# Engines in source order, weights split two batches ahead, metered side work, and turns on GpSimd's queue

## The chip, the core and the metric

The kernel runs on one core of a Trainium2 chip. The metric is the device time of one execution in microseconds (us). The engines are PE (TensorE, matmuls and transposes), DVE (VectorE), ACT (ScalarE), POOL (GpSimd) and SP (SyncE, which here only issues DMAs). All run their own instruction streams and wait for each other at semaphores.

## The reference

One decoder layer for 256 rows of 2048 columns, in float32:

```python
x = x + 0.5 * swiglu(rms_norm(x, ffn1_norm), gate1, up1, down1)     # 2048 -> 5632 -> 2048
h = rms_norm(x, mix_norm)
fq, fk, fv, f_logit, sq, sk, sv, mq = split(h @ w_in)
out_a = forgetting_attention(norm(fq), norm(fk), fv, log_sigmoid(f_logit + bias))  # 6 heads, causal
out_b = sliding_window_sink_attention(norm(sq), norm(sk), sv, sinks, slopes)       # 6 heads, 2 kv heads
mn = rms_norm(mem, mem_norm)
out_c = memory_attention(norm(mq), norm(mn @ w_mem_k), mn @ w_mem_v)               # 4 heads
x = x + concat(out_a, out_b, out_c) @ w_out
x = x + 0.5 * swiglu(rms_norm(x, ffn2_norm), gate2, up2, down2)
```

## The kernel before

**Projections.** Every weight matrix is read once, in batches of two K tiles (`KB = 2`) by 512 or 384 columns. A batch is loaded by a DMA of SP (`raw_`, four tiles), rounded by ACT to `hi_` and subtracted by DVE to `lo_` (three tiles each, L218 to L221), and PE forms hi x hi, hi x lo and lo x hi for two row tiles and two K tiles: 12 matmuls (`mm_rows`, L315 to L317). The two accumulators in PSUM (tag `acc`) alternate between the chunks of columns. The stages are FFN1 (chunks `ag`, `au` for gate and up, `ad` for down), the mix stage, and FFN2 (`bg`, `bu`, `bd`). The mix stage projects the memory's keys and values (`mk`, `mv`), then the columns of `w_in` in the chunks mq, sqa, skv, sqb, fqa, fka, fqb, fkb, fva, fvb, then `w_out` (`wo`).

**Side work.** After each batch `lanes.tick()` advances generators one step: a `yield n` says in how many ticks the next step comes. Two lanes hold a PSUM tile each for attention pairs (fox pairs f0, f2, f4; window pairs w0, w2, w4; memory pairs m0, m2); free generators do the rest. `heads_T` normalises the heads of a chunk (ACT squares, a chain of small DVE instructions, ACT scaling into `q_...`), transposes them with PE into the chunk's own PSUM tile (L565) and copies them out by ACT (L567). The probabilities `ss_` of a pair are transposed by PE into `pt_` (L717, L783).

**Turns.** Where a larger tile is transposed without PE (the rows of x, the hidden activations of the FFNs, the memory), DVE transposes blocks of 32 x 32 within the tile (`turn_out`, L262), four DMAs write it to DRAM (`far_`, L268), and one reads it back in the order wanted (`turn_in`). SP issues these DMAs, in one queue with the weight loads.

**Order.** Only the opening is in `tc.manual_schedule()`; from the first chunk's batch at `k == 6` on, the framework's scheduler places each engine's instructions by its own estimate of when they are ready, so a step written later can stand earlier.

Of the kernel before, what the change touches and what calls it, by code (L numbers as in the profile page):

```python
# [1 line left out]

# [31 lines left out]
class Lanes:  # L34
# [12 lines left out]
    def run(self, name, gen):  # L47
        self.free.append([name, gen, 0])

    def _step(self, item):  # L50
        item[2] -= 1
        if item[2] > 0:
            return True
        try:
            item[2] = next(item[1])
            return True
        except StopIteration:
            self.done.add(item[0])
            return False

    def tick(self):
        self.free = [i for i in self.free if self._step(i)]
        started = False
        for n in range(2):
            if self.lane[n] is None and not started:
                for q in self.queue:
                    if all(d in self.done for d in q[2]):
                        self.queue.remove(q)
                        self.lane[n] = [q[0], q[1](f"l{n}"), 0]
                        started = True  # L70
                        break
            if self.lane[n] is not None and not self._step(self.lane[n]):
                self.lane[n] = None

    def finish(self, *names):
        while not all(n in self.done for n in names):
            self.tick()
# [3 lines left out]
def hybrid_layer(ctx, tc, x, mem, ffn1_norm, ffn1_gate, ffn1_up, ffn1_down, mix_norm, mem_norm,  # L81
# [27 lines left out]
    opening = ExitStack()  # L109
    opening.enter_context(tc.manual_schedule())  # L110
# [4 lines left out]
    graw1 = cpool.tile([NK, P], F32, name="graw1")  # L115
# [15 lines left out]
    ones = cpool.tile([P, P], F32, name="ones")  # L131
    nc.gpsimd.memset(ones, 1.0)
    warm = cpool.tile([P, 1], F32, name="warm")
    nc.scalar.activation(warm, ones[:, 0:1], AF.Silu)
# [18 lines left out]
    tri = tri3[:, 0:P]  # L153
# [3 lines left out]
    def constants(tag):  # L157
# [34 lines left out]
        tc.keep_in_program_order(  # L192
            nc.vector.tensor_scalar(out=nsink6, in0=sink6, scalar1=-1.0, scalar2=None, op0=ALU.mult))
# [19 lines left out]
    def load_w(w, k0, nk, c0, width, name):  # L213
        raw = wpool.tile([P, KB, 512], F32, tag="raw", bufs=4, name=f"raw_{name}")
        hi = wpool.tile([P, KB, 512], F32R, tag="hi", bufs=3, name=f"hi_{name}")
        lo = wpool.tile([P, KB, 512], F32R, tag="lo", bufs=3, name=f"lo_{name}")
        r, h, l = (t[:, :nk, :width] for t in (raw, hi, lo))
        nc.sync.dma_start(  # L218
            r, w[k0 * P:(k0 + nk) * P, c0:c0 + width].rearrange("(k p) c -> p k c", p=P))
        nc.scalar.copy(h, r)  # L220
        nc.vector.tensor_tensor(out=l, in0=r, in1=h.bitcast(F32), op=ALU.subtract)  # L221
        return h, l

# [32 lines left out]
    def turn_out(tmp, src, name):  # L256
# [3 lines left out]
        for t in range(NT):  # L260
            tc.keep_in_program_order(
                nc.vector.transpose(  # L262
                    out=tmp.rearrange("p (t b k s) -> p t k b s", b=4, t=NT, s=32)[:, t],
                    in_=src[:, t, :].rearrange("p (k b f) -> p k b f", b=4, f=32)))
        yield 2
        far = dpool.tile([NT, 4, 32, 4, P], F32, name=f"far_{name}")
# [3 lines left out]
        yield 2  # L270
# [5 lines left out]
    def turned(dst):  # L276

        return dst.rearrange("p (c k s) -> p k c s", c=4 * NT, s=32)

    def scaled(xT, raw, k0, g0):  # L280

        rv = turned(raw)
        for k in range(4):
            g = gT[:, g0 + k0 + k:g0 + k0 + k + 1]
# [4 lines left out]
            if k % 2:  # L289
                yield 1  # L290

    def turn_chunk(xT, src, tile, k0, g0, name):
        far = yield from turn_out(tile(f"out_{name}"), src, name)
        raw = tile(f"in_{name}")
        nc.sync.dma_start(*turn_in(raw, far))
        yield 3
        yield from scaled(xT, raw, k0, g0)

    def square_sums(ss, src, c):
        for t in range(NT):  # L300
            junk = small.tile([P, 512], F32, tag="junk", bufs=2, name="junk")
            tc.keep_in_program_order(
                nc.scalar.activation(junk, src[:, t, :], AF.Square, accum_out=ss[:, t, c:c + 1]))
# [15 lines left out]
    def project(acc, aT, w, c0, width, kts, nk_all, done, name, before=None):  # L319

        for k0, n in kts:
            k = k0
            while k < k0 + n:
                b = min(KB, k0 + n - k)
                if before:
                    before(k)
                wh, wl = load_w(w, k, b, c0, width, f"{name}_{k}")
                for j in range(b):
                    mm_rows(acc, aT, k + j, wh[:, j, :], wl[:, j, :], done == 0, done == nk_all - 1)
                    done += 1  # L330
                k += b
                lanes.tick()
        return done

    def project_end(acc, aT, w, c0, k0, n, name, landed):
# [3 lines left out]
        for k in range(k0, k0 + n, KB):  # L339
            wh, wl = load_w(w, k, KB, c0, 512, f"{name}_{k}")  # L340
# [9 lines left out]
        lanes.tick()  # L350

    def project_first(acc, aT, w, x_tiles, ordered, name):
# [11 lines left out]
        def batch(k):  # L364
            if k in XLOAD:
                load_x(nc.sync, *XLOAD[k])
            return load_w(w, k, KB, 0, 512, f"{name}_{k}")

# [10 lines left out]
        lanes.tick()  # L379
        two, three = split_one(2), split_one(3)  # L380
        mm_rows(acc, aT, 2, *two, False, False)
        nxt = batch(4)
        x_tiles(4)
        mm_rows(acc, aT, 3, *three, False, False)
        lanes.tick()
        for k in range(4, NK, KB):
            (wh, wl), nxt = nxt, batch(k + KB) if k + KB < NK else None
            if k == 6:
                ordered()
# [3 lines left out]
            lanes.tick()  # L393


    def ffn(xT, before, first, stats, wg, wu, wd, after, beside, last, name):


        with tc.tile_pool(name=f"h_{name}", bufs=1, reuse_waits="tile") as hpool, \
# [68 lines left out]

    ss0 = cpool.tile([P, NT, 4], F32, name="ss0")
# [6 lines left out]
    XLOAD.update({6: (6, 2), 8: (8, 4), 10: (12, 4)})  # L476
# [11 lines left out]
    def sum_stages(ss, src, c, wait=None):  # L488
        yield 2 + c if wait is None else wait
# [13 lines left out]
    def turns_a(htmp, turn_tile):  # L503
# [3 lines left out]
        for c in range(4):  # L507
# [24 lines left out]
    ffn(x0T, None, (x_tiles, opening.close), stats0, gate1, up1, down1, after1, beside_a, False, "a")  # L532
# [3 lines left out]
    with tc.tile_pool(name="mix", bufs=1, reuse_waits="tile") as mx, \  # L536
# [3 lines left out]
        def heads_T(acc, nh, r, gi, dst, name, off=0):  # L540

            q = mt.tile([P, 4 * SEQ], F32, tag="q", name=f"q_{name}").rearrange("p (t w) -> p t w", t=NT)
            s = small.tile([P, NT, 4], F32, tag="hs", name=f"hs_{name}")
            cols = lambda h: slice(off + h * HD, off + (h + 1) * HD)
            nc.vector.memset(s, 1.0)
            for t in range(NT):
                for h in range(nh):
                    junk = small.tile([P, HD], F32, tag="junkh", bufs=2, name="junkh")
                    nc.scalar.activation(junk, acc[:, t, cols(h)], AF.Square, scale=r[:, t:t + 1],
                                         accum_out=s[:, t, h:h + 1])  # L550
                yield 1
# [4 lines left out]
            yield 2  # L556
# [4 lines left out]
            yield 2  # L561
            tv = acc.rearrange("p a b -> p (a b)")[:, :nh * SEQ].rearrange("p (h s) -> p h s", h=nh)
            for h in range(nh):
                for t in range(NT):
                    nc.tensor.transpose(tv[:, h, t * P:(t + 1) * P], q[:, t, h * HD:(h + 1) * HD], ident)  # L565
# [340 lines left out]
```

## Time and profile before

| | us |
|---|---|
| median of 3 runs (range) | 1803.91 (1803.52 to 1804.58) |
| the profiled execution | 1803.99 |
| span of its trace | 1802.3 |
| PE busy | 1792.4 |
| DVE busy | 976.4 |
| ACT busy | 845.7 |
| POOL busy | 12.1 |

The span is what the trace covers, from the first to the last instruction; the 1.7 us beyond it lie around the execution. Busy time of an engine is the sum over its instructions. The granted clock of PE is full in all slices.

### The profile page before, as it was taken

What the parts mean: (1) busy time and instruction counts of PE and PEld (TensorE: products, weight loads), DVE (VectorE), ACT (ScalarE), POOL (GpSimd) and SP (SyncE); (2) the same over time, 40 slices, a digit from 0 to 9 for tenths busy, and PEclk for the clock granted to TensorE, in tenths of its full rate; (3) what the DMA queues carried; (4) which work ended last, traced back from release to release, by engine and by line L of the source; (5) the groups of instructions that cost most, each with busy time, mean ns of one, the idle gap of its engine ahead of it and who ended that gap; (6) DMA issues with size and microseconds to landing.
All of it is one profiled execution on the core that took longest, in us unless ns stands there. A gap on an engine that the chain in (4) does not pass through costs nothing.

```text
span 1802.3 us, 21677 instructions
## 1 busy us (share of the span) xinstructions
PE 1792.4 (99%) x8170; PEld 1507.2 (84%) x8170; DVE 976.4 (54%) x1197; ACT 845.7 (47%) x1149; POOL 12.1 (1%) x31
## 2 busy tenths in 40 slices
PE   9999999999999999999999999999999999999998
PEld 7888888888888888888999888888888888888887
DVE  5555555555555564645665565555555555544443
ACT  6444444444445443656666454444444444433332
POOL 2000000000000000000000000000000000000000
PEclk9999999999999999999999999999999999999999
DMA  7777777777787777765656586777777777666663
GB/s 240 217 219 214 220 214 218 217 216 218 227 252 234 231 220 239 223 176 152 183 151 185 176 257 188 217 216 222 222 225 223 217 219 214 218 200 198 206 205 128
DMA packets 228025, 379.16 MB, mean 210 GB/s; under 512 B 13834, under 2 KB 65360, under 8 KB 227792
## 3 DMA queue, kind: packets, MB, share of 16 engines
q1 hardware_dynamic: 226512, 375.36, 68.8%
q8 instruction: 64, 1.05, 0.2%
q0 software_dynamic: 528, 1.22, 0.2%
q10 hardware_dynamic: 880, 1.19, 0.2%
q14 instruction: 41, 0.34, 0.1%
HBM read 358.31 MB, written 19.41 MB: 210 GB/s over the span
## 4 chain that ended last, share of the span: by engine, by line
PE 98%; DVE 1%; ACT 1%; DMA 0%; issue 0%; POOL 0%; DVEq 0%; POOLq 0%; ACTq 0%
PE ua L316 4%; PE ua L317 4%; PE gb L317 4%; PE ub L317 4%; PE gb L315 4%; PE ub L315 4%; PE gb L316 4%; PE ub L316 4%; PE ua L315 4%; PE da L316 4%; PE db L316 4%; PE db L315 4%; PE da L317 4%; PE db L317 4%; PE da L315 4%; PE ga L316 4%
## 5 line engine op out<-in xcount | busy, mean ns | idle before, releaser
L221 DVE TENSOR_TENSOR lo_bd<-raw_bd,hi_bd 128x1024 fp32r<-128x1024 f32 x88 | 107.7, 1224 | 122.6 <-ACT hi_bd L220 122.5
L221 DVE TENSOR_TENSOR lo_bu<-raw_bu,hi_bu 128x1024 fp32r<-128x1024 f32 x88 | 107.8, 1225 | 119.5 <-ACT hi_bu L220 119.5
L221 DVE TENSOR_TENSOR lo_au<-raw_au,hi_au 128x1024 fp32r<-128x1024 f32 x88 | 107.8, 1225 | 114.2 <-ACT hi_au L220 114.2
L221 DVE TENSOR_TENSOR lo_ad<-raw_ad,hi_ad 128x1024 fp32r<-128x1024 f32 x88 | 107.5, 1223 | 104.7 <-ACT hi_ad L220 104.6
L220 ACT CAST hi_bd<-raw_bd 128x1024 fp32r<-128x1024 f32 x88 | 92.8, 1055 | 145.5 <-PE db L317 140.5
L221 DVE TENSOR_TENSOR lo_bg<-raw_bg,hi_bg 128x1024 fp32r<-128x1024 f32 x88 | 107.4, 1220 | 96.4 <-ACT hi_bg L220 95.6
L220 ACT CAST hi_bg<-raw_bg 128x1024 fp32r<-128x1024 f32 x88 | 92.8, 1055 | 142.1 <-PE gb L317 86.5
L221 DVE TENSOR_TENSOR lo_ag<-raw_ag,hi_ag 128x1024 fp32r<-128x1024 f32 x86 | 104.9, 1220 | 93.8 <-ACT hi_ag L220 92.9
L220 ACT CAST hi_ad<-raw_ad 128x1024 fp32r<-128x1024 f32 x88 | 92.8, 1054 | 131.7 <-PE da L317 121.5
L220 ACT CAST hi_ag<-raw_ag 128x1024 fp32r<-128x1024 f32 x86 | 90.7, 1055 | 135.9 <-PE ga L317 83.2
L220 ACT CAST hi_bu<-raw_bu 128x1024 fp32r<-128x1024 f32 x88 | 92.8, 1054 | 105.2 <-PE ub L317 78.9
L220 ACT CAST hi_au<-raw_au 128x1024 fp32r<-128x1024 f32 x88 | 92.5, 1054 | 102.6 <-PE ua L317 79.1
L316 PE MATMUL da<-lo_ad,hT_a 128*128 128x512 f32 x352 | 137.0, 389 | 0.8 <-DVE lo_ad L221 0.8
L316 PE MATMUL ua<-lo_au,x0T 128*128 128x512 f32 x352 | 137.0, 389 | 0.3 <-DVE lo_au L221 0.3
L316 PE MATMUL gb<-lo_bg,x2T 128*128 128x512 f32 x352 | 137.0, 389 | 0.0
L315 PE MATMUL gb<-hi_bg,x2T 128*128 128x512 f32 x352 | 136.9, 389 | 0.0
L317 PE MATMUL ua<-hi_au,x0T 128*128 128x512 f32 x352 | 136.9, 389 | 0.0
L315 PE MATMUL da<-hi_ad,hT_a 128*128 128x512 f32 x352 | 136.9, 389 | 0.0
L317 PE MATMUL da<-hi_ad,hT_a 128*128 128x512 f32 x352 | 136.9, 389 | 0.0
L317 PE MATMUL gb<-hi_bg,x2T 128*128 128x512 f32 x352 | 136.9, 389 | 0.0
L315 PE MATMUL ub<-hi_bu,x2T 128*128 128x512 f32 x352 | 136.9, 389 | 0.0
L316 PE MATMUL ub<-lo_bu,x2T 128*128 128x512 f32 x352 | 136.9, 389 | 0.0
(478 smaller groups left out, 3934.9 us busy)
## 6 DMA issues: line engine op xcount, KB each, us to landing
raw_au<-in_ffn_up_dram SPq DMA_DIRECT2D x88, 512.0 KB, 4.5
raw_ad<-in_ffn_down_dram SPq DMA_DIRECT2D x88, 512.0 KB, 5.0
raw_bg<-in_ffn_gate_dram SPq DMA_DIRECT2D x88, 512.0 KB, 4.5
raw_bu<-in_ffn_up_dram SPq DMA_DIRECT2D x88, 512.0 KB, 4.4
raw_bd<-in_ffn_down_dram SPq DMA_DIRECT2D x88, 512.0 KB, 4.6
raw_ag<-in_ffn_gate_dram SPq DMA_DIRECT2D x86, 512.0 KB, 4.5
raw_wo<-in_w_out_dram SPq DMA_DIRECT2D x16, 512.0 KB, 5.2
far_a<-turn_out_a SPq DMA_DIRECT2D x44, 128.0 KB, 2.6
```

The source lines that it names most:

```text
L220: nc.scalar.copy(h, r)
L221: nc.vector.tensor_tensor(out=l, in0=r, in1=h.bitcast(F32), op=ALU.subtract)
L315: nc.tensor.matmul(acc[:, t, :w], hi, wh, start=first, stop=False)
L316: nc.tensor.matmul(acc[:, t, :w], hi, wl, start=False, stop=False)
L317: nc.tensor.matmul(acc[:, t, :w], lo, wh, start=False, stop=last)
```

## The change

It has five parts. (1) The whole program is in `manual_schedule()`, so each engine runs in the order in which the code is written. (2) A list `plan` holds all weight batches in order, and `weights()` loads and splits them ahead of use: one batch ahead at first, two from the first chunk's `k == 8` on. (3) The steps of side work carry estimates of their DVE and ACT cost; a tick has some room for each, by the width of the batch, and a step that would overdraw it is put off. `Slots` hands out the shared tiles, and `held_by` makes a chunk's start wait until the steps that read its accumulator are written. (4) A turn's five DMAs are issued by POOL, and the reader follows six ticks after the turn. (5) The heads of all chunks but fkb, and the probabilities of m0, m2, w0 and w2, are transposed by turns instead of PE; fkb, w4 and the fox pairs stay on PE.

```diff
     def _step(self, item):
         item[2] -= 1
-        if item[2] > 0:
+        if item[2] > 0 or any(cost and room <= -0.4 for cost, room in zip(item[3], self.room)):
             return True
+        self.room = [room - cost for cost, room in zip(item[3], self.room)]
...
-    def tick(self):
-        self.free = [i for i in self.free if self._step(i)]
+    def tick(self, room=(0.0, 0.0)):
+        self.room = [min(a + b, b) for a, b in zip(self.room, room)]
...
+        self.free = [i for i in self.free if self._step(i)]
...
-    opening = ExitStack()
-    opening.enter_context(tc.manual_schedule())
+    ctx.enter_context(tc.manual_schedule())
...
+    AHEAD = [1]
+    plan, traced = [], []
...
+    def weights(name, k):
+
+        while plan and len(traced) < 1 + AHEAD[0]:
+            traced.append((plan[0][4], plan[0][1], load_w(*plan.pop(0))))
+        got = traced.pop(0)
+        assert got[:2] == (name, k), (got[:2], name, k)
+        return got[2]
+
+    def room(width):
+        t = KB * 6 * (width + 32) / 2400
+        return t - 0.17 - 1.03e-3 * KB * width, t - 0.22 - 0.81e-3 * KB * width
...
-            nc.sync.dma_start(far[:, :, :, a, :].rearrange("t b f n -> f (t b) n"),
-                              tmp[32 * a:32 * a + 32, :].rearrange("f (c n) -> f c n", n=P))
-        yield 2
+            nc.gpsimd.dma_start(far[:, :, :, a, :].rearrange("t b f n -> f (t b) n"),
+                                tmp[32 * a:32 * a + 32, :].rearrange("f (c n) -> f c n", n=n))
         return far
 
     def turn_in(dst, far):
-        return dst.rearrange("p (t n) -> p t n", t=NT), far.rearrange("t b f a n -> (b f) t (a n)")
...
+        nt, n = far.shape[0], far.shape[4]
+        nc.gpsimd.dma_start(dst[:, 0:nt * 4 * n].rearrange("p (t n) -> p t n", t=nt),
+                            far.rearrange("t b f a n -> (b f) t (a n)"))
...
-                wh, wl = load_w(w, k, b, c0, width, f"{name}_{k}")
-                for j in range(b):
+                wh, wl = weights(name, k)
+                for j in range(KB):
                     mm_rows(acc, aT, k + j, wh[:, j, :], wl[:, j, :], done == 0, done == nk_all - 1)
                     done += 1
-                k += b
-                lanes.tick()
+                k += KB
+                lanes.tick(room(width))
...
         for k in range(4, NK, KB):
-            (wh, wl), nxt = nxt, batch(k + KB) if k + KB < NK else None
-            if k == 6:
-                ordered()
+            if k == 8:
+                AHEAD[0] = 2
+            wh, wl = weights(name, k)
...
+        def turn(src, name, out, then=None):
+
+            i, tmp = yield from take("turn", f"turn_{name}")
+            yield 0, 0.17 + 1.05e-3 * src.shape[1] * src.shape[2], 0.0
+            turn_in(tmp, turn_out(tmp, src, name))
+            if then:
+                then()
+            yield 5
+            yield from out(tmp)
+            slots["turn"].give(i)
...
-            tv = acc.rearrange("p a b -> p (a b)")[:, :nh * SEQ].rearrange("p (h s) -> p h s", h=nh)
-            for h in range(nh):
-                for t in range(NT):
-                    nc.tensor.transpose(tv[:, h, t * P:(t + 1) * P], q[:, t, h * HD:(h + 1) * HD], ident)
+            if not by_pe:
+                lanes.done.add(f"{name}.acc")
             yield 1
-            nc.scalar.activation(dst, tv, AF.Copy, scale=gT[:, G_HEAD + gi:G_HEAD + gi + 1])
+            if by_pe:
+                tv = acc.rearrange("p a b -> p (a b)")[:, :nh * SEQ].rearrange("p (h s) -> p h s", h=nh)
+                for h in range(nh):
+                    for t in range(NT):
+                        nc.tensor.transpose(tv[:, h, t * P:(t + 1) * P], q[:, t, h * HD:(h + 1) * HD], ident)
+                slots["q"].give(iq)
+                yield 1, 0.0, 0.8
+                nc.scalar.activation(dst, tv, AF.Copy, scale=gain)
+                lanes.done.add(f"{name}.acc")
+                return
+
+            def out(tmp):
+                yield 0, 0.0, 0.8
+                nc.scalar.activation(dst.rearrange("p h (c s) -> p h c s", s=32), turned(tmp, NT, nh), AF.Copy,
+                                     scale=gain)
+
+            yield from turn(q, name, out, lambda: slots["q"].give(iq))
...
+        held_by = [("mk.acc",), ("mv",)]
 
         def chunk(c0, width, name):
+            lanes.finish(*held_by[-2])
             acc = psum("acc", name)
             project(acc, x1T, w_in, c0, width, [(0, NK)], NK, 0, name)
+            held_by.append(("sv", "sk.acc") if name == "skv" else (name if name[:2] == "fv" else f"{name}.acc",))
             return acc
```

The probabilities by DMA use the same `turn` (`turn_p`), followed by an ACT copy back into `ss_`.

What the change does to the order shows at three places. The first is PE in chunk fqb, between two weight batches (`hi_fqb`, `lo_fqb`; x1T are the normalised rows). Before, the six transposes of fka's heads stand there:

```order
L315 MATMUL fqb<-hi_fqb_7309,x1T 128x384
L316 MATMUL fqb<-lo_fqb_7310,x1T 128x384
L317 MATMUL fqb<-hi_fqb_7309,x1T 128x384
L565 MATMUL fka<-ident,q_fka 128x128 x6
L315 MATMUL fqb<-hi_fqb_7333,x1T 128x384
L316 MATMUL fqb<-lo_fqb_7334,x1T 128x384
L317 MATMUL fqb<-hi_fqb_7333,x1T 128x384
```

After, the batches follow each other directly:

```order
L354 MATMUL fqb<-hi_fqb_7238,x1T 128x384
L355 MATMUL fqb<-lo_fqb_7239,x1T 128x384
L356 MATMUL fqb<-hi_fqb_7238,x1T 128x384
L354 MATMUL fqb<-hi_fqb_7256,x1T 128x384
L355 MATMUL fqb<-lo_fqb_7257,x1T 128x384
L356 MATMUL fqb<-hi_fqb_7256,x1T 128x384
```

The six transposes are gone from PE, and the heads of fka go out by a turn. Over the program 78 such instructions go: eight each for mk, mq, m0 and m2, six each for sqa, sqb, fqa, fka, fqb, w0 and w2, four for sk.

The second place is PE at the heads of fkb, which stay on PE. Before, their transposes stand inside chunk fva, with 12 more matmuls of fva and 8 of a fox pair ahead of fvb:

```order
L315 MATMUL fva<-hi_fva_7743,x1T 128x384
L316 MATMUL fva<-lo_fva_7744,x1T 128x384
L317 MATMUL fva<-hi_fva_7743,x1T 128x384
L565 MATMUL fkb<-ident,q_fkb 128x128 x6
L315 MATMUL fva<-hi_fva_7767,x1T 128x384
L316 MATMUL fva<-lo_fva_7768,x1T 128x384
```

After, they stand behind the last matmul of fva, directly ahead of fvb:

```order
L354 MATMUL fva<-hi_fva_7701,x1T 128x384
L355 MATMUL fva<-lo_fva_7702,x1T 128x384
L356 MATMUL fva<-hi_fva_7701,x1T 128x384
L648 MATMUL fkb<-ident,q_fkb 128x128 x6
L354 MATMUL fvb<-hi_fvb_7744,x1T 128x384
L355 MATMUL fvb<-lo_fvb_7745,x1T 128x384
L356 MATMUL fvb<-hi_fvb_7744,x1T 128x384
```

fvb takes the accumulator that fkb held, and ACT copies fkb's transposed heads out of it (`qkv<-fkb`), so the matmuls that lay between are no longer there.

The third place is DVE at the end of FFN1's third down chunk, where it adds the chunk to x (`x_sb<-da`) and transposes x's blocks for a turn (`turn_out_x`). Before:

```order
L221 TENSOR_TENSOR lo_ad_42_4985<-raw_ad_42_4983,hi_ad_42_4984 128x1024
L221 TENSOR_TENSOR lo_ad_0_5010<-raw_ad_0_5008,hi_ad_0_5009 128x1024
L450 SCALAR_TENSOR_TENSOR x_sb<-da_4552,x_sb 128x512 x2
L262 STREAM_TRANSPOSE turn_out_x_5026<-x_sb 128x4x4x32 x2
L221 TENSOR_TENSOR lo_ad_2_5031<-raw_ad_2_5029,hi_ad_2_5030 128x1024
L221 TENSOR_TENSOR lo_ad_4_5049<-raw_ad_4_5047,hi_ad_4_5048 128x1024
```

After:

```order
L264 TENSOR_TENSOR lo_ad_0_4969<-raw_ad_0_4967,hi_ad_0_4968 128x1024
L264 TENSOR_TENSOR lo_ad_2_4987<-raw_ad_2_4985,hi_ad_2_4986 128x1024
L484 SCALAR_TENSOR_TENSOR x_sb<-da_4562,x_sb 128x512 x2
L264 TENSOR_TENSOR lo_ad_4_5012<-raw_ad_4_5010,hi_ad_4_5011 128x1024
L302 STREAM_TRANSPOSE turn_out_x_5028<-x_sb 128x4x4x32 x2
L264 TENSOR_TENSOR lo_ad_6_5038<-raw_ad_6_5036,hi_ad_6_5037 128x1024
```

The split of the next chunk's second batch (`lo_ad_2`) now stands ahead of the sum, and one more split between the sum and the block transposes.

## Rows read from the trace of the kernel before

**Rows 1.** The page: span; engines' busy us; a group: busy us, mean ns, idle.

```profile
span 1802.3 us, 21677 instructions
PE 1792.4 (99%) x8170; PEld 1507.2 (84%) x8170; DVE 976.4 (54%) x1197; ACT 845.7 (47%) x1149; POOL 12.1 (1%) x31
...
L316 PE MATMUL da<-lo_ad,hT_a 128*128 128x512 f32 x352 | 137.0, 389 | 0.8 <-DVE lo_ad L221 0.8
```

**Rows 2.** Windows: length; PE, PEld, DVE, ACT, POOL busy (count); clock; DMA share, GB/s.

```profile
200.00:400.00 200.00, 200.00 (x884) 165.62 (x883) 105.66 (x100) 88.77 (x94) 0.00 (x0) 1.00 0.72 215
...
850.00:900.00 50.00, 50.00 (x295) 48.61 (x294) 32.85 (x86) 32.61 (x84) 1.11 (x2) 1.00 0.66 184
```

**Rows 3.** The chain that ended last: start, us, what.

```profile
813.94 0.87 PE mq L565 x8
...
862.70 0.44 PE skv L565 x4
...
924.07 0.66 PE fka L565 x6
924.72 0.17 PE fqb L315
...
925.94 0.17 PE fqb L316
...
962.66 0.65 PE fkb L565 x6
```

**Rows 4.** PE's waits: line, releaser, us in total, times, longest.

```profile
PE db L345 <- DVE x_sb L450: 0.8, 1, 0.8
...
PE wo L316 <- DVE lo_wo L221: 0.6, 1, 0.6
PE sqa L316 <- DVE lo_sqa L221: 0.5, 1, 0.5
PE ua L316 <- DVE lo_au L221: 0.3, 1, 0.3
```

**Rows 5.** Timeline, 671 to 675 us: start, us, instruction, idle before it and releaser.

```profile
671.18 1.29 DVE L450 SCALAR_TENSOR_TENSOR x_sb<-da,x_sb 128x512 f32<-128x512 f32 x2 [3.01 <-PE da L317]
...
672.38 1.30 DVE L262 STREAM_TRANSPOSE turn_out_x<-x_sb 128x512 f32<-128x512 f32 x2
...
673.60 2.32 DVE L221 TENSOR_TENSOR lo_ad<-raw_ad,hi_ad 128x1024 fp32r<-128x1024 f32 x2
...
674.84 0.50 PE L316 MATMUL da<-lo_ad,hT_a 128*128 128x512 f32 x1 [0.76 <-DVE lo_ad L221]
```

**Rows 6.** Timeline, SP's DMA issues in `wo`, 1044 to 1048 us.

```profile
1044.07 0.37 SPq L295 DMA_DIRECT2D turn_in_x<-far_x  x1
...
1044.48 3.96 SPq L218 DMA_DIRECT2D raw_wo<-in_w_out_dram  x3
```

**Rows 7.** Timeline, ACT, around the transposes of fkb.

```profile
962.70 0.83 ACT L220 CAST hi_fvb<-raw_fvb 128x768 fp32r<-128x768 f32 x1 [1.25 <-PE fva L317]
...
963.44 0.90 ACT L567 ACTIVATE qkv<-fkb,gT 128x768 f32<-128x768 f32 x1
```

**Rows 8.** DMA issues: queue, count, KB each, median us to landing.

```profile
far_x<-turn_out_x SPq DMA_DIRECT2D x28, 128.0 KB, 3.1
...
turn_in_m<-far_m SPq DMA_DIRECT2D x4, 512.0 KB, 6.0
```

**Rows 9.** Groups of POOL's instructions: busy us, mean ns, idle before.

```profile
L660 POOL DMA_DIRECT2D nck_all<-nck_dram x1 | 0.6, 577 | 3.2 <-ACT junkh L549 3.2
L162 POOL DMA_DIRECT2D bias<-in_forget_bias_dram x1 | 0.6, 569 | 1.1 <-DMA graw<-in_mem_norm_dram 1.1
...
L161 POOL DMA_DIRECT2D graw<-in_fox_q_gain_dram x1 | 0.5, 487 | 0.0
```

**Rows 10.** Groups of DVE, 760 to 980 us: busy us, mean ns, idle before.

```profile
L631 DVE TENSOR_SCALAR ss_f<-ss_f,ri_f 128x256 f32<-128x256 f32 x6 | 2.1, 349 | 0.0
...
L631 DVE TENSOR_SCALAR ss_f<-ss_f,ri_f 128x128 f32<-128x128 f32 x6 | 1.7, 285 | 0.1
```

More of the change, by code (lines that the diff above doesn't have):

```diff
@@ L1 @@
-from contextlib import ExitStack
 import concourse.bass as bass
@@ L73, in tick, with __init__, take, give @@
                 self.lane[n] = None
+        self.free = [i for i in self.free if self._step(i)]
     def finish(self, *names):
         while not all(n in self.done for n in names):
-            self.tick()
+            self.tick((1.2, 1.2))
+class Slots:
+    def __init__(self, n):
+        self.n, self.asked, self.taken, self.back = n, 0, 0, set()
+    def take(self):
+        i, self.asked = self.asked, self.asked + 1
+        while self.taken < i or i >= self.n and i - self.n not in self.back:
+            yield 1
+        self.taken += 1
+        return i
+    def give(self, i):
+        self.back.add(i)
 @with_exitstack
@@ L466, in xchunk, with plan_ffn @@
         return x_sb[:, :, c * 512:(c + 1) * 512]
+    def plan_ffn(wg, wu, wd, name, first):
+        for j in range(DFF // 512):
+            for w, kind in ((wg, "g"), (wu, "u")):
+                k0 = 4 if first and j == 0 and w is wg else 0
+                plan_w(w, j * 512, 512, k0, NK - k0, f"{name}{kind}{j}")
+        for c in range(4):
+            plan_w(wd, c * 512, 512, 0, NF, f"{name}d{c}")
+    W_IN = [(MEM_Q, 512, "mq"), (FOX_F, 390, "sqa"), (SWA_K, 512, "skv"), (SWA_Q + 384, 384, "sqb")]
+    for half, a in (("a", 0), ("b", 384)):
+        W_IN += [(FOX_Q + a, 384, f"fq{half}"), (FOX_K + a, 384, f"fk{half}")]
+    W_IN += [(FOX_V, 384, "fva"), (FOX_V + 384, 384, "fvb")]
+    W_OUT = [(0, 6, 10), (1, 6, 10), (0, 0, 6), (1, 0, 6), (2, 0, 16), (3, 0, 16)]
+    plan_ffn(gate1, up1, down1, "a", True)
+    plan_w(w_mem_k, 0, 512, 0, NK, "mk")
+    plan_w(w_mem_v, 0, 512, 0, NK, "mv")
+    for c0, width, n in W_IN:
+        plan_w(w_in, c0, width, 0, NK, n)
+    for c, k0, n in W_OUT:
+        plan_w(w_out, c * 512, 512, k0, n, f"wo{c}")
+    plan_ffn(gate2, up2, down2, "b", False)
     ss0 = cpool.tile([P, NT, 4], F32, name="ss0")
@@ new lines, in by_dma, with transposes @@
+            def by_dma():
+                yield from probabilities()
+                yield 1
+                yield from turn_p(s, f"p_{name}")
+            def transposes(tag):
+                pp = psum(tag, f"pt_{name}")
+                for i in range(2):
+                    for j in range(3):
+                        nc.tensor.transpose(pp[:, i, j * P:(j + 1) * P], s[:, i, j * P:(j + 1) * P], ident)
+                yield 1, 0.0, 0.85
+                nc.scalar.copy(s, pp[:, :, 0:3 * P])
@@ L725, in values @@
+            if by_pe:
+                lanes.run(f"e_{name}", probabilities())
+                lanes.put(f"p_{name}", transposes, (f"e_{name}",))
+            else:
+                lanes.run(f"p_{name}", by_dma())
         def values(tag, h0, v, mix0, name):
@@ L790, in mem_stages @@
[L790 to L797 removed]
+                    nc.scalar.activation(part(i, t), sp[:, i, t * SEQ:(t + 1) * SEQ].rearrange(
+                        "p (k s) -> p k s", k=2), AF.Exp, bias=nm[:, i, t:t + 1], accum_out=sm[:, t, i:i + 1])
@@ new lines, in rest, with mem_values, stages @@
+            def rest():
+                yield 1, 1.7, 0.0
+                normalise(part, sm, name)
+                yield 1
+                yield from turn_p(s, f"p_{name}")
+            lanes.run(f"p_{name}", rest())
+        def mem_values(h0):
+            def stages(tag):
+                name = f"m{h0}"
+                pT = pTs[name]
+                po = psum(tag, f"o_{name}")
+                for i in range(2):
+                    for k in range(2):
+                        nc.tensor.matmul(po[:, i, 0:SEQ], mv[:, k, (h0 + i) * HD:(h0 + i + 1) * HD],
+                                         pT[:, i, k * SEQ:(k + 1) * SEQ], start=k == 0, stop=k == 1)
+                yield 1, 0.7, 0.6
+                put_heads(12 + h0, po)
+                slots["s"].give(held[name])
+            return stages
```

327 lines of the change are left out of this document (163 added, 164 removed).

## The prediction

> **What bounds the kernel now.** I read the page first: TensorE (PE) is busy 1792.4 of 1802.3 us [rows 1], so little other than its own instruction list can be shortened. The windows say the same stage by stage: 884 matmuls fill 200 us of FFN1, 0.2262 us each; in the mix stage PE has 50.00 us of work in 50, VectorE (DVE) 32.85 and ScalarE (ACT) 32.61, all at the full granted clock [rows 2]. A batch of twelve 512-column matmuls is thus T = 2.71 us. In a 384-column chunk seven matmuls start from 924.72 to 925.94, 0.174 us each, and T = 2.09 us [rows 3]. Next came the chain that ended last, to price what a removed PE instruction gives back: eight transposes take 0.87 us of it, six 0.66, four 0.44 [rows 3], always 0.11 each, with projection matmuls close up on both sides. Last, PE's waits: 0.8 us for `lo_ad`, 0.6 for `lo_wo`, 0.5 for `lo_sqa`, 0.3 for `lo_au`, and 0.8 at the kernel's end for `x_sb` [rows 1, 4]. Each is short by about 0.16 us: idle time counts from a matmul's modelled end, 0.389 us after its start [rows 1], while in a stream the next one starts after 0.226.
>
> **Transposes removed.** The orders differ by exactly 78 PE transposes: eight each for mk, mq and the two memory pairs, six each for sqa, sqb, fqa, fka, fqb, w0 and w2, four for sk. By the chain's rows that is 4 x 0.87 + 7 x 0.66 + 0.44 = 8.54 us. The whole gain is real only if PE has a batch of split weights ready each time it goes straight on; that is the next part. What replaces them is off PE: 14 more DVE stream transposes (0.65 us each [rows 5]) and five DMA issues per turn on GpSimd (POOL), whose queue now holds nothing else there. DVE at 33 us in 50 has room for these 9 us over the whole stage [rows 2].
>
> **Waits removed.** `lo_ad` at 674.84: DVE had put `x_sb` (1.29 us) and two stream transposes (1.30) ahead of the split [rows 5]. The order of after has one split between the two and starts two batches ahead. `lo_wo` at 1048: SP issued `turn_in_x` ahead of three weight loads [rows 6]; without turns on SP the loads lie up to four tiles ahead. `lo_sqa` and `lo_au` are splits too, and a lead of two batches, 4.2 to 5.4 us, is eight times the longer wait. I take all four: 0.8 + 0.6 + 0.5 + 0.3 + 4 x 0.16 = 2.84 us (bounds 0 and 2.84). The wait at the end stays.
>
> **Wait added at fkb.** Before, the fkb transposes stand inside fva with work behind them. After, they are followed at once by fvb, which writes the PSUM tile that the transposes filled; so PE waits for ACT's copy of it. The transposes end at 962.66 + 0.65 = 963.31, the copy starts at 963.44 and takes 0.90 [rows 3, 7]. PE follows a releaser within 0.08 us (the first of two splits from 673.60, half of 2.32 long, and PE at 674.84 [rows 5]). That is 963.31 to 964.42, 1.1 us. If the ACT work queued ahead (a weight split of 0.83 [rows 7] and a cast of the same order) is late, up to 2.7. I take 1.2: ACT is only busy two thirds of the stage [rows 2].
>
> **Late turns.** A turn is four far DMAs and one back. `far_x` landed in 3.1 us and `turn_in_m`, the slowest turn back, in 6.0 [rows 8]; issues of POOL with up to 128 rows took 487 to 577 ns [rows 9]. With issue price p the turn takes 5p + 9.1, 11.9 us at 0.55. After the source yields 5, ACT's consumer stands six ticks behind: 6 x 2.09 = 12.5 us in a 384-column chunk, less DVE's transposes and a split ahead of them, three quarters of 1.30 and some 1.0, so ACT waits from 10.5 us on. Its next weight split is then late, but PE needs that two batches later: 4.2 less split (0.83), its DVE half (about 1) and the consumer itself (0.9), 1.5 us of slack [rows 5, 7]. So PE waits once a turn is longer than 12.0 us, and in 512-column chunks, by the same steps, than about 16. Six turns consume in 384-column batches (p_m0, p_m2, sk, sqb, p_w0, fka). Late per turn: 5p - 2.9. At 577 ns it is nothing; if the issue grows with rows as from one (487 ns) to 128 (569), the 256 rows of a turn cost 651 ns, 0.36 us a turn, 2.1 in all. I take 0.6, nearer to nothing, because 577 ns was paid for the largest transfer (1152 KB), and keep 0 to 2.1.
>
> **Source order.** Side work on PE (logits, values, remaining transposes) now stands where it was written, often one tick behind the ACT or DVE step it reads. Those engines run up to two batches ahead, which hides a step of 1 to 3 us but not always. Nothing in the trace of before shows this; below, it is nothing (the metering postpones the work), above I put eight interludes at half a microsecond, 4. I take 0.5.
>
> **The sum**, against the profiled run's own 1803.99 us: - 8.54 - 2.84 + 1.2 + 0.6 + 0.5 = 1794.91. The run lies 0.08 above the median of 1803.91: 1794.8 us.
>
> [...] The trace shows 0.064 us for 128 more elements of a TENSOR_SCALAR [rows 10], 0.5 ns each, against 1.1 ns in the weight split (1.16 us for 1024 [rows 5]): only the first kind runs at the doubled rate. [...]
>
> **Rivals.** (1) *Turns starve or source order stalls, and most of the gain is returned.* [...] Six turns late by 1 to 2 us give 6 to 12 less the 3 or so that metering and splits already ahead can absorb, or the source order takes its 4 us: 1797.5 to 1803, about 1800. [...] Chance 0.15.
> (2) *Slower: GpSimd's price per issue doubles at 256 rows.* At p = 1.1 a tight turn is 2.6 us late, six are 15.6: 1794.2 + 15.6 = 1809.8. It ends above the border of 1807.6 from p = 1.03 on. Against: 127 more rows cost 82 ns. Chance 0.08.
> (3) *All new waits are hidden*, fkb's too, if side work that tick order postpones puts something between: 1803.91 - 8.54 - 2.84 = 1792.5, and below it only if gaps under the tenth of a microsecond that the waits' view lists close up as well. For it: PE's idle time is 10 us in all [rows 1]. Against: PSUM has two accumulators, and fvb takes the one that fkb held. Chance 0.07.
> That the transposes are not gone is excluded by the order.
>
> **How the numbers follow.** The forecast holds 0.70, with its own range from 1792.5 (as rival 3, its floor) to 1797.5 (1803.91 - 8.54 - 2.84 + 2.7 at fkb + 2.1 for turns, rounded up). For 8 in 10 I go from 1791.5 to 1801, which leaves out rival 2, the upper part of rival 1 (0.06) and half of rival 3 (0.04). Runs of this kernel spread by 0.06%, and 0.2%, 3.6 us, is about what can be told from no change. Faster than 1800.3 takes the forecast, rival 3 and a third of rival 1: 0.82. Within it lies the rest of rival 1: 0.10. Slower is rival 2: 0.08.
>
> **What would show it.** PE's waits without `lo_ad`, `lo_wo`, `lo_sqa`, `lo_au`; fqb, mv and the other chunks whose matmuls follow with no transposes between; a new wait of about 1.1 us of fvb on ACT's `qkv` copy; POOL issues near 0.58 us and at most 0.4 us of PE wait behind each tight turn. PE waits for `hi_` or `lo_` tiles right behind a turn's consumer would show rivals 1 and 2 (a long issue, the second). I am wrong if POOL's issue is well over 0.65 us, if the turns' DMAs land later than SP's did, or if PE's interludes wait for DVE or ACT several microseconds in all.

## The result and the profile after

The changed kernel takes 1830.58 us (median of 4 runs, 1828.35 to 1834.73) against 1804.19 of the kernel before (4 runs): 1.0149 times, with a 95% interval of 1.013 to 1.0168. The forecast was 1794.8 us, with a range up to 1801. It is 26 us slower, and 36 above the forecast.

The page of the changed kernel, which answers to [rows 1]:

```profile
span 1826.6 us, 21784 instructions
...
PE 1794.4 (98%) x8092; PEld 1501.4 (82%) x8092; DVE 992.7 (54%) x1217; ACT 851.9 (47%) x1149; POOL 149.1 (8%) x256
```

PE has 78 instructions less and yet counts as busy 2 us longer; its idle time went from 10 to 32 us. Its waits (line, releaser, total us, times, longest):

```profile
PE db L354 <- ACT hi_bd L263: 7.4, 3, 3.5
PE tp_x L278 <- DVE x_sb L989: 3.2, 1, 3.2
PE db L355 <- DVE lo_bd L264: 2.0, 3, 0.8
PE o_m L921 <- ACT ss_m L777: 1.8, 1, 1.8
PE mk L355 <- DVE lo_mk L264: 1.7, 1, 1.7
...
PE fvb L354 <- ACT qkv L651: 1.0, 1, 1.0
PE fqb L354 <- ACT hi_fqb L263: 1.0, 1, 1.0
PE s_w L788 <- ACT qkv L657: 1.0, 1, 1.0
PE fva L354 <- ACT hi_fva L263: 0.9, 1, 0.9
...
PE o_w L857 <- ACT ss_w L777: 0.9, 1, 0.9
...
PE ub L355 <- DVE lo_bu L264: 0.8, 1, 0.8
```

Against [rows 4], `lo_ad` and `lo_wo` are gone, as forecast. New are waits in three groups: in FFN2's down stage (`db`), at the last x2 chunk (`tp_x`), and spread over the mix stage. The largest is read from windows of 60 us around the three ends of `db` chunks (us; PE, PEld, DVE, ACT, POOL with counts; granted clock; DMA share; GB/s):

```profile
1622.00:1682.00 60.00, 57.25 (x252) 46.82 (x251) 27.01 (x23) 21.65 (x22) 0.00 (x0) 1.00 0.63 201
1689.00:1749.00 60.00, 56.08 (x234) 45.48 (x233) 24.83 (x22) 20.38 (x20) 0.00 (x0) 0.94 0.63 202
1753.00:1813.00 60.00, 57.26 (x245) 46.69 (x244) 26.43 (x23) 21.07 (x20) 0.00 (x0) 0.97 0.57 184
```

At 0.2262 us each, 60 us hold 265 matmuls. Missing are 13, 31 and 20, 64 x 0.2262 = 14.5 us, although the idle time listed is only 9.4. Of the other 5.1 about 1.0 is the 0.16 us that the list leaves out of each of the six waits. The rest is PE's clock after the waits of the second and third end, the 0.94 and 0.97; at the first end it stays full, and the 13 are idle time alone. The timeline at the first of the three shows what was late:

```profile
1626.48 1.29 DVE L484 SCALAR_TENSOR_TENSOR x_sb<-db,x_sb 128x512 f32<-128x512 f32 x2 [0.41 <-PE db L356]
...
1627.20 0.36 SPq L1002 DMA_DIRECT2D out_dram<-x_sb  x1
...
1627.65 7.81 SPq L246 DMA_DIRECT2D raw_bd<-in_ffn_down_dram  x5
...
1632.77 1.04 ACT L263 CAST hi_bd<-raw_bd 128x1024 fp32r<-128x1024 f32 x1 [7.96 <-DMA raw_bd<-in_ffn_down_dram]
```

SP stores the finished chunk of x only when DVE has added it, and the next weight load follows 0.45 us behind the store. It lands 5 us later; ACT has by then waited 7.96 us, and PE has used up its two batches. The order on SP's queue says why. The names hold the chunk and its K tile (`bd1_4` is the third batch of the second chunk). Before:

```
L218 DMA raw_bd1_10_12609<-in_ffn2_down_dram 128x2x512
L868 DMA out_0_dram<-x_sb_78 128x512
L218 DMA raw_bd1_12_12627<-in_ffn2_down_dram 128x2x512
```

After:

```
L246 DMA raw_bd1_2_12524<-in_ffn2_down_dram 128x2x512
L1002 DMA out_0_dram<-x_sb_78 128x512
L246 DMA raw_bd1_4_12547<-in_ffn2_down_dram 128x2x512
```

Six loads of the next chunk stood ahead of the store, now two. SP's own waits at the three stores (before, 1600 to 1760 us, and after, 1600 to 1780) show the same: it stood 0.7 us at each, and now stands 11.6, while the loads behind are not issued.

```profile
SPq L868 <- DVE x_sb L450: 2.1, 3, 0.7
```

```profile
SPq L1002 <- DVE x_sb L484: 34.8, 3, 11.6
```

In the mix stage, a turn with its reader (DVE's transposes, POOL's issues, ACT's copy back) reads:

```profile
851.27 1.24 DVE L302 STREAM_TRANSPOSE turn_p_m<-ss_m 128x1024 f32<-128x1024 f32 x1
...
852.80 0.58 POOL L306 DMA_DIRECT2D far_p_m<-turn_p_m  x1 [6.84 <-DVE turn_p_m L302]
...
854.64 1.63 POOL L306 DMA_DIRECT2D far_p_m<-turn_p_m  x3 [1.25 <-issue]
...
859.98 0.56 POOL L312 DMA_DIRECT2D turn_p_m<-far_p_m  x1 [3.71 <-DMA far_p_m<-turn_p_m]
...
866.37 1.04 ACT L777 COPY ss_m<-turn_p_m 128x1024 f32<-128x1024 f32 x1 [2.33 <-DMA turn_p_m<-far_p_m]
```

From 852.5, the end of the transposes, to 866.37 are 13.9 us, where 12.0 were allowed for; ACT idles 2.33 and PE's `o_m` behind it 1.8. In this turn 1.25 of the 1.9 us are a pause of POOL between its first and second issue, for which the profile names no releaser. The same 1.25 us stand at this issue in a_store_pool, c_es, d_sum and e_late below, so it is no chance of one run. Groups of POOL and the DMA issues show the turns in general:

```profile
L306 POOL DMA_DIRECT2D far_a<-turn_out_a x44 | 25.6, 587 | 397.2 <-DVE turn_out_a L302 397.0 <-issue 0.2
...
L312 POOL DMA_DIRECT2D turn_in_a<-far_a x11 | 7.9, 720 | 60.8 <-DMA far_a<-turn_out_a 54.8 <-ACT hi_ad L263 6.0
```

```profile
far_a<-turn_out_a POOLq DMA_DIRECT2D x44, 128.0 KB, 4.9
turn_in_a<-far_a POOLq DMA_DIRECT2D x11, 512.0 KB, 5.2
```

An issue costs 587 or 720 ns, the four far ones within the forecast's 0.55 to 0.65. What it had wrong is the far DMA's landing, 4.9 us instead of 3.1 [rows 8].

ACT's and DVE's source order shows in the window pairs' exponentials:

```profile
911.01 0.96 DVE L264 TENSOR_TENSOR lo_fqb<-raw_fqb,hi_fqb 128x768 fp32r<-128x768 f32 x1 [1.08 <-ACT hi_fqb L263]
911.89 0.16 DVE L220 TENSOR_SCALAR v_fka<-hs_fka 128x8 f32<-128x8 f32 x1
...
914.41 0.15 DVE L820 TENSOR_TENSOR es_w<-nm_w,sink 128x4 f32<-128x4 f32 x1
914.60 0.21 ACT L823 ACTIVATE es_w<-es_w 128x4 f32<-128x4 f32 x1 [3.62 <-DVE es_w L820]
...
916.47 1.55 ACT L263 CAST hi_fqb<-raw_fqb 128x768 fp32r<-128x768 f32 x2
```

ACT waits 3.62 us for an addition of 0.15, because DVE reaches it behind a chain of 14 small instructions for other heads; ACT's weight cast stands behind the exponentials, and PE waits 1.0 us for `hi_fqb`.

### The profile page after: what moved, and what is told of

Its sections match the earlier page's. It is cut to its first block, busy times and chain, and to the rows that moved or that the text cites. A ratio compares the mean times of both kernels' runs of the same rounds, so it can differ in the third digit from the quotient of the medians.

```text
span 1826.6 us, 21784 instructions
## 1 busy us (share of the span) xinstructions
PE 1794.4 (98%) x8092; PEld 1501.4 (82%) x8092; DVE 992.7 (54%) x1217; ACT 851.9 (47%) x1149; POOL 149.1 (8%) x256
## 4 chain that ended last, share of the span: by engine, by line
PE 91%; DMA 4%; DVE 2%; ACT 2%; issue 1%; POOL 0%; SPq 0%; DVEq 0%; ACTq 0%; POOLq 0%
PE gb L355 4%; PE gb L354 4%; PE gb L356 4%; PE da L356 4%; PE ub L355 4%; PE da L354 4%; PE da L355 4%; PE ub L356 4%; PE ub L354 4%; PE ua L355 4%; PE ua L354 4%; PE ua L356 4%; PE db L355 4%; PE db L356 4%; PE ga L355 4%; PE ga L356 4%
## 5 line engine op out<-in xcount | busy, mean ns | idle before, releaser
L354 PE MATMUL db<-hi_bd,hT_b 128*128 128x512 f32 x348 | 137.7, 396 | 7.4 <-ACT hi_bd L263 7.4
L355 PE MATMUL db<-lo_bd,hT_b 128*128 128x512 f32 x348 | 137.4, 395 | 2.0 <-DVE lo_bd L264 2.0
L356 PE MATMUL db<-hi_bd,hT_b 128*128 128x512 f32 x348 | 137.0, 394 | 0.0
```

What stands on the lines that cost most here:

```text
L354: nc.tensor.matmul(acc[:, t, :w], hi, wh, start=first, stop=False)
L355: nc.tensor.matmul(acc[:, t, :w], hi, wl, start=False, stop=False)
L356: nc.tensor.matmul(acc[:, t, :w], lo, wh, start=False, stop=last)
```

## The experiments

All times are medians in us; the kernel before ran beside each group (1803.88, 1804.53, 1804.09, 1804.21).

**Stores off SP's queue (a_store_pool).**

```diff
-        (nc.sync, nc.scalar)[t ^ (c0 > 0)].dma_start(ov[:, t, cols], x_sb[:, t, cols])
+        (nc.gpsimd if c < 3 else nc.sync, nc.scalar)[t ^ (c0 > 0)].dma_start(ov[:, t, cols], x_sb[:, t, cols])
```

> The changed kernel, with those stores of x's first three chunks in FFN2 that SP issued moved to GpSimd. Theory 1: three waits of PE for hi_bd in FFN2's down stage, with the slow matmuls behind them, come from SP's queue: in source order a store that waits for x_sb stands ahead of the weight loads. Then these waits go and PE's excess after 1600 us falls from about 16 us to about 1: 1815 us, 13 to 16 less than the changed kernel. Rival: the loads are late because two batches ahead is too short for a load of 4.8 us there; then the time stays within 2 us of 1830.

1810.78 (1809.25 to 1812.38; 1.0038 of before, 1.0023 to 1.0053): 19.8 less than the changed kernel. The window of the first chunk end is full again:

```profile
1622.00:1682.00 60.00, 60.00 (x267) 49.67 (x266) 28.32 (x25) 23.12 (x22) 0.59 (x1) 1.00 0.63 204
```

The `db` waits for `hi_bd` and `lo_bd` are gone. The profiled spans differ by 18.9 us (1826.6 and 1807.7), 15.5 of it in FFN2's down stage (the table below). The wait at `tp_x` fell as well, from 3.2 to 1.6 us, at a place that the edit does not touch, so a part of this difference is chance of the two profiled runs.

**Turns with two more ticks (a_turn7).**

```diff
-            yield 5
+            yield 7
```

> The changed kernel, with the reader of a mix-stage turn eight ticks behind it instead of six. Theory 2: late turns hold ACT and through it PE (o_m, o_w, one s_w, and the transposes of the last x2 chunk, about 10 us with the slow matmuls). Then these waits go and the time falls by 7 to 10 us, to about 1822. Rival: the waits in the mix stage come from ACT and DVE standing in source order behind each other's small steps (es_w, the rsqrt chains); then at most 2 us are gained, and the other waits stay.

1830.69 (1829.93 to 1831.88), no gain. `o_m`, `o_w` and `s_w` no longer wait, but these do:

```profile
PE fqa L354 <- ACT q_sk L639: 4.0, 1, 4.0
...
PE pt_f L842 <- DVE ss_f L735: 1.9, 1, 1.9
PE pt_w L842 <- DVE ss_w L735: 1.5, 1, 1.5
```

The turns were late, but a later reader pushes back what shares its tiles and accumulators, so the theory's remedy falls.

**Only the turns' queue, in the kernel before (b_pool).**

```diff
-            nc.sync.dma_start(far[:, :, :, a, :].rearrange("t b f n -> f (t b) n"),
+            nc.gpsimd.dma_start(far[:, :, :, a, :].rearrange("t b f n -> f (t b) n"),
...
-        nc.sync.dma_start(*turn_in(raw, far))
+        nc.gpsimd.dma_start(*turn_in(raw, far))
```

> The kernel before, with nothing changed but that GpSimd issues the turns' DMAs (four far, one back) instead of SP. Theory: GpSimd's queue costs little by itself: the turns are 3 to 4 us longer, but the scheduled order has room, and the wait for lo_wo goes: 1802 to 1805 us. [...]

1804.71 (10 runs; 1.0003, 0.9994 to 1.0012). GpSimd's queue by itself costs and gives nothing that can be told, although a far DMA lands 4.7 us after issue there too; `lo_wo` no longer waits.

**Only source order, in the kernel before (b_order).**

```diff
-    opening = ExitStack()
-    opening.enter_context(tc.manual_schedule())
+    ctx.enter_context(tc.manual_schedule())
...
```

(and the calls that close the opening's block or keep single instructions in order, which are then needless)

> The kernel before, with all of its program in source order and nothing else changed (one batch is loaded and split at its use, no batch ahead). Theory: source order needs the splits ahead; without them PE waits for nearly every batch (a load of 4.5 us less what the four raw tiles hide, then 1.05 + 1.2 us of splits against 2.7 us of matmuls): well above 1830, 1900 or more. Rival: source order by itself costs only the stores' waits and the side work's: about 1830.

2152.25 (1.1914, 1.1863 to 1.1966): part (1) cannot stand alone. The time is as the theory said, the places are not: PE does not wait for nearly every batch, its three largest rows list 21, 20 and 11 waits in stages of 88 batches. SP stands 131 us in total at the far DMAs of FFN1's turns and as long at FFN2's, so this run does not tell the missing lead from the turns on SP's queue, which c_turn_sp tests.

**One batch ahead (c_ahead1)**, with the stores off SP:

```diff
-                AHEAD[0] = 2
+                AHEAD[0] = 1
```

> a_store_pool with one weight batch loaded and split ahead instead of two. The forecast put the loss of the old waits down to the second batch ahead. Theory: in source order the lead is what pays for every step of side work on ACT and DVE, so that with half of it each step in the mix stage shows: 1840 or more. Rival: the second batch ahead is not needed: within 3 us of 1810.8.

1848.00 (1846.94 to 1850.0): the second batch is worth 37 us.

**Turns on SP in source order (c_turn_sp)**, with the stores off SP:

```diff
-            nc.gpsimd.dma_start(far[:, :, :, a, :].rearrange("t b f n -> f (t b) n"),
+            nc.sync.dma_start(far[:, :, :, a, :].rearrange("t b f n -> f (t b) n"),
```

(and `turn_in` alike)

> a_store_pool with the turns' DMAs on SP's queue again. Theory: in source order turn_in waits at the head of SP's queue for its far DMAs (about 2.6 us) with weight loads behind it, and the stores showed that two batches ahead do not cover a load held up there: 33 turns, some microseconds each, well above 1830. Rival: four raw tiles cover 5 us, as they did before: 1806 to 1812, and shorter turns take away some late waits.

2242.26 (1.2436, 1.2413 to 1.246), slower even than b_order with no batch ahead. SP's own waits name the cause, and it is not quite the theory's: it stands 11.7 us a turn at the first far DMA until DVE has transposed, with loads behind (2.6 us at most at the turns of `turn_out_a` and `turn_out_b` in the kernel before), and only about 2 at `turn_in`. The kernel has 45 turns, not 33.

```profile
SPq L306 <- DVE turn_out_a L302: 129.2, 11, 12.1
SPq L306 <- DVE turn_out_b L302: 128.8, 11, 11.7
```

So the queue that is worth nothing in the scheduled kernel is what makes source order possible here.

**Heads back on PE (c_heads_pe)**, with the stores off SP: `by_pe=True` in all calls of `heads_T`, for example

```diff
-        lanes.run("mk", heads_T(acc, 4, rm, 5, mkT, "mk"), True)
+        lanes.run("mk", heads_T(acc, 4, rm, 5, mkT, "mk", by_pe=True), True)
```

> a_store_pool with the heads of all chunks transposed by PE again (50 of the 78 transposes), the probabilities of m0, m2, w0, w2 still by turns. By the forecast's price that is 50 x 0.11 = 5.5 us more, and each chunk behind may wait for ACT's copy as fvb does for fkb's (1.1 us each, at most 7): 1814 to 1822. Rival (the turns of the heads cost as much in late waits as they save): within 2 us of 1810.8, or less.

1840.84 (1836.81 to 1844.25): 30 us more, far above both theories. The profiled runs are 27.1 us apart: PE idles 12.4 us more and is busy 14.7 more, 5.5 of it for the transposes; the rest goes with a granted clock of 0.993 instead of 1.000. The longest two waits are

```profile
PE fqa L648 <- ACT q_fqa L639: 4.2, 1, 4.2
PE o_m L921 <- ACT ss_m L777: 4.1, 1, 4.1
```

In source order a PE transpose waits for its heads with the projections behind it (9.8 us in all), and the next chunk but one for the copy (`fqb` and `sqb`, 4.7).

**No metering (c_noroom)**, with the stores off SP:

```diff
-        if item[2] > 0 or any(cost and room <= -0.4 for cost, room in zip(item[3], self.room)):
+        if item[2] > 0 or any(cost and room <= -99.0 for cost, room in zip(item[3], self.room)):
```

> a_store_pool without the metering: a step of side work is never put off, whatever its DVE and ACT cost. Theory: metering keeps several long steps from one batch, so without it more splits in the mix stage are late: 1815 to 1825. Rival: it does nothing that the two batches of lead do not cover, or its delays are themselves what makes turns late: 1806 to 1812.

1819.22 (1816.87 to 1820.49): metering gives 8.4 us.

**The es addition earlier (c_es)**, with the stores off SP: the three lines that make `es` move from `probabilities()` to the step that makes `nm`.

```diff
                                         op=ALU.min)
+                es = small.tile([P, NT, 2], F32, tag="es", name=f"es_{name}")
+                nc.vector.tensor_tensor(out=es, in0=nm,
+                                        in1=sink6[:, None, h0:h0 + 2].to_broadcast([P, NT, 2]),
+                                        op=ALU.add)
```

> a_store_pool with one small DVE addition per window pair (es, the sink's logit) written in the step before, where nm is made, instead of at the head of the exponentials. Theory 3: ACT stands in source order behind it (3.4 to 3.6 us a pair, since DVE reaches it only behind an rsqrt chain or weight splits), and that makes PE's waits for hi_fqb and hi_fva and the lo_ waits and slow matmuls behind them, 4.6 us in all. Then these go: about 1806.5 us. Rival: the next thing in ACT's queue (nm's reduction, the turn's landing) is as late; then under 1 us is gained.

1806.39 (10 runs; 1.0008, 0.9999 to 1.0018): 4.4 us less than a_store_pool, as expected; every run lies below all of a_store_pool's. The waits for `hi_fqb` and `lo_fqb` and the one at `s_w` are gone, and those for fva are 0.6 each.

**The row-scale chains elsewhere (c_rstd)**, with the stores off SP:

```diff
-        rm = row_rstd(ssm, "mem")
+        rm = stat["mem"]
...
-        r1s = row_rstd(ss1, "x1")
         acc = psum("acc", "mk")
         project(acc, memT, w_mem_k, 0, 512, [(0, NK)], NK, 0, "mk")
+        r1s = row_rstd(ss1, "x1")
```

(the memory's is computed at the end of its turns, x2's at batch 14 of the first gate chunk)

> a_store_pool with the three row-scale chains of DVE (13 small instructions each) written elsewhere: the memory's at the end of its turns in FFN1, x1's behind chunk mk, x2's one batch earlier and before the gate's activation. Theory 4: in source order a chain stands ahead of the weight splits of the next stage and makes PE's waits for lo_mk (1.9 us) and for hi_bu and lo_bu (1.5 us): 3.4 us less, 1807.4. Rival: the chain behind mk delays mv's splits in the same way; then under 1.5 us.

1810.63 (9 runs, 1806.54 to 1813.88), by itself inconclusive: `lo_mk`, `hi_bu` and `lo_bu` no longer wait, but in the profiled run (1813.88, its slowest) `tp_x` waits 2.8 and `o_m` 2.4 us, more than in a_store_pool.

**Both (d_sum).** The two edits together on a_store_pool.

> a_store_pool with the edits of c_es and of c_rstd together. If both causes are as named they add up: 1810.8 - 4.4 (c_es) - 3.5 (the waits that left c_rstd's trace) = 1803 us, with the late turns (o_m, tp_x, s_w, s_f: some 5 to 9 us in the traces so far) still there. Rival: they share their waits, or moving the chains makes turns late (c_rstd's median did not fall): 1806.

1803.15 (11 runs; 0.9998, 0.9989 to 1.0008), the expected value; so the chains are worth 3.2 us beside c_es by the medians. The two intervals overlap, so that this size is less sure than that the waits for `lo_mk`, `hi_bu` and `lo_bu` are gone here too.

**Later readers for x2 and the memory pairs (d_wait7)**, on d_sum:

```diff
-            yield 5
+            yield 7 if name[:2] in ("x2", "p_") and name[2:3] != "w" else 5
```

> d_sum with the readers of the x2 turns and of the memory pairs' turns two ticks later. If late turns still cost at o_m (1.2 to 2.7 us) and at the last x2 chunk's transposes (1.8 to 5 us), the time falls by 3 to 6 us and spreads less: 1798 to 1800. Rival (a later reader only moves the wait, as in a_turn7): no change beyond 1 us.

1802.96 (11 runs): the rival. `o_m` no longer waits, and at x2 `gb` waits for splits instead (0.8 and 0.7).

**fkb by a turn too (d_fkb)**, on d_wait7:

```diff
-                lanes.run(name, heads_T(acc, 3, r1s, g, dst[:, a:b, :], name, by_pe=name == "fkb"), True)
+                lanes.run(name, heads_T(acc, 3, r1s, g, dst[:, a:b, :], name), True)
```

> d_wait7 with the heads of fkb turned by DMA as well. The wait of fvb for ACT's copy (1.15 us) and six transposes (0.66) go: 1.8 us less than d_wait7. Rival: the last fox pairs' logits, now up to ten ticks later, come to stand in front of w_out's late part or behind a late turn: same or more.

1801.72 (11 runs; 0.9988, 0.9979 to 0.9996): 1.2 less of the 1.8 expected, and the wait of fvb is gone.

**The last x2 chunk's transposes later (e_late)**, on d_fkb:

```diff
+        def after_turns(tag):
+            yield 3
+            yield from transpose_chunk(lambda: x2T, lambda: xchunk(3), 12, 4, G_FFN2, "x2_3")(tag)
...
-                lanes.put(f"bT{c}", transpose_chunk(lambda: x2T, lambda: xchunk(3), 12, 4, G_FFN2, "x2_3"))
+                lanes.put(f"bT{c}", after_turns)
```

> d_fkb with the PE transposes of x2's last chunk one weight batch later. In d_fkb's trace PE still waits there for x_sb (1.3 us), and then twice for weight splits (1.5 us and 0.8 of slow pace behind) that the same side work delays. If the first wait is only a matter of place, it goes and 1.3 to 3 us with it: 1799 to 1800.5. Rival: DVE and ACT are late as a whole there, since the last turn lands late, and PE waits for the splits instead: within 1 us of 1801.7.

1797.87 (6 runs; 0.9966, 0.9954 to 0.9978): 3.9 less, more than the 1.3 to 3 expected; the fastest here, below the kernel before by 0.34%. What PE still waits for between the opening and the tail:

```profile
PE ua L355 <- DVE lo_au L264: 0.8, 1, 0.8
PE fva L354 <- ACT hi_fva L263: 0.6, 1, 0.6
PE fva L355 <- DVE lo_fva L264: 0.6, 1, 0.6
PE sqa L355 <- DVE lo_sqa L264: 0.5, 1, 0.5
PE fka L354 <- ACT q_sqb L641: 0.4, 1, 0.4
PE pt_w L844 <- DVE ss_w L737: 0.3, 1, 0.3
```

## Why the prediction was wrong

The step that failed is "Source order", costed at 0.5 us with 4 as its upper bound. It looked for PE's side work alone, and PE's waits of before could not show what the scheduler had been hiding on the other queues. Where the time went shows by stage, from the first matmul of one to that of the next (us):

| | opening and FFN1 | mix | FFN2, gate and up | FFN2, down |
|---|---|---|---|---|
| before | 731.9 | 346.0 | 479.7 | 244.7 |
| after | 730.2 | 354.7 | 481.5 | 260.2 |
| a_store_pool | 730.3 | 352.3 | 480.4 | 244.7 |
| e_late | 732.1 | 339.5 | 479.6 | 244.8 |

Three things were missing:

- *SP.* "without turns on SP the loads lie up to four tiles ahead" is wrong: in source order a load stands on SP where its batch is split, two batches ahead, behind whatever was written earlier. The stores of x were such a thing: moving them gave 19.8 us, and the down stage its 244.7 us back. No term of the sum held them.
- *ACT and DVE behind each other.* The es addition cost 4.4 us (c_es), the three row-scale chains about 3 (d_sum); when each was moved its waits were gone.
- *PE's order.* The transposes of the last x2 chunk stood right behind the sum of DVE that they read. One batch later they no longer wait, nor do the splits behind them, and the time falls by 3.9 us (e_late).

From the changed kernel to e_late that is 19.8 + 4.4 + 3.2 + 0.2 + 1.2 + 3.9 = 32.7 us. The 0.2 of d_wait7 is no change, and the 1.2 of d_fkb is no part of the 35.8 that the forecast missed, which had counted the wait at fkb. So about 31 of the 35.8 are found. The other 4 or 5 are near the 3.2 us of waits that e_late lists, with 0.16 hidden in each of the six.

*Transposes removed* held as a count. The price of 0.11 us no run isolates, but the mix stage bears it out: in e_late it is 6.5 us shorter than before with 84 transposes (9.2 us) less, and its waits come to some 1.8 us more. (The turns add 20 block transposes of DVE, not 14; no term hung on that.) But the step took "a batch of split weights ready" for granted, and c_heads_pe shows that in source order the heads on PE would cost 30 us, not 5.5: leaving them to turns was worth more than the forecast said, for another reason.

*Waits removed*: `lo_ad` and `lo_wo` went, `lo_sqa` stayed at 0.5, and `lo_au` rose from 0.3 to 0.8: 1.7 of the 2.84 us came, less that 0.5. There a lead of two batches was not enough.

*Wait at fkb*: 1.2 forecast; 1.0 listed, with 0.16 hidden 1.2. Right.

*Late turns*: 0.6 forecast. `o_m` and `o_w` waited 2.7 us in all behind turns at whose landing ACT stood. Part of the 3.2 at `tp_x` is of the same kind, behind the last x2 turn, which the term had not counted. ACT's line ahead of `o_m` is shown above; those ahead of `o_w` and `tp_x` are

```profile
933.00 0.83 ACT L777 COPY ss_w<-turn_p_w 128x768 f32<-128x768 f32 x1 [3.28 <-DMA turn_p_w<-far_p_w]
...
1080.93 1.70 ACT L327 ACTIVATE x2T<-turn_x,gT 128x256 fp32r<-128x256 f32 x4 [2.21 <-DMA turn_x<-far_x]
```

The 1.0 at `s_w` looks alike and is none: ACT did not stand at its turn, and the wait went with c_es. The issue price was right, the landing of the far DMAs (4.9 for 3.1) was not. A landing is counted from the start of its issue, so the forecast's 5p + 9.1 held two issues twice, 1.1 us, which hid a part of that. It is luck that its limit of 12.0 us fits the turn shown (13.9 less the 1.8 of `o_m`): PE did not wait for a weight split behind the reader, as the forecast had it, but for the reader itself. Later readers took the waits at `o_m` away, but not the time (a_turn7, d_wait7).

*The rivals.* The first (source order takes 4 us, about 1800) had the kind and not the size. The second, a doubled issue price, is refuted: 587 and 720 ns. Six turns late by 1 to 2 us, which the first counts as well, no run shows: the longest issue of a turn in the changed kernel took 0.75 us, and behind late turns of the mix stage PE waited at two places, 1.8 us at `o_m` and 0.9 at `o_w`. A busy DVE alone does not explain POOL's pauses: one of 1.14 us in the same kernel, ahead of an issue of `far_m` (534.67 to 535.80 us), falls into a time in which DVE idles until 535.63. The third, all new waits hidden, is refuted by the wait at fkb.

`tp_x` and `o_m` vary between kernels by 1 to 2 us at places that an edit does not touch, and the traces say with what. `o_m` waits 0.5 us less than ACT stands at the landing of its turn: 2.33 and 1.8 in the changed kernel, 1.76 and 1.2 in a_store_pool, 3.20 and 2.7 in c_es, 2.90 and 2.4 in c_rstd. In the kernels that load two batches ahead and leave `tp_x` at its place, it waits 1.3 to 1.6 us where ACT stands no more than 0.2 at the last x2 turn, and 2.3 to 3.2 where it stands 1.28 to 2.21.

What stays open: why the landings vary (the median of `turn_x` is 4.9 us in a_store_pool and 6.8 in c_rstd), and what POOL's pauses are.

## What to carry to other kernels

Before an order that a scheduler made is replaced by source order, go through every queue, the DMA-issuing ones first, and ask of each instruction that waits for a late result (a store, a turn) what is written behind it; the trace of before shows at most that such an instruction waits (0.7 us at each store), not what it would hold up, because other work stands ahead of it there. In this kernel a lead of two batches did not cover a store at the end of a chunk with a load of 5 us behind it. Price a removed instruction by what it would wait for in the new order, not only by its own length.

## What the runs showed of the hardware

After a wait of 3.45 us PE came back at a slower pace: the matmuls of 512 columns start 0.43 us apart instead of 0.226, at a granted clock of 0.50 from 1700.4 to 1704.6 us (0.94 over the whole window).

```profile
1698.53 0.79 PE L354 MATMUL db<-hi_bd,hT_b 128*128 128x512 f32 x1 [3.45 <-ACT hi_bd L263]
...
1700.38 0.63 PE L356 MATMUL db<-hi_bd,hT_b 128*128 128x512 f32 x1
1700.80 0.63 PE L354 MATMUL db<-hi_bd,hT_b 128*128 128x512 f32 x1
```

So a wait of a few microseconds can cost more than its length: the three ends of `db` chunks list 9.4 us of idle time and lose 14.5. It need not: waits of 1.99 and 0.76 us at the first end left the clock full, and waits of 1.98 and 0.76 at the third brought seven starts 0.43 us apart. And a far DMA of 128 KB issued by GpSimd landed 4.9 us after its issue (`far_a`), the same one by SP 2.6 in the kernel before.
